# A two-layer hybrid decoder trunk in fp32: spacing of attention's units among the weight blocks of the input projection, 1.65 against 2.3 blocks

## The chip, the cores and the metric

The kernel runs on one core of a Trainium2 chip. Its engines are TensorE (PE: matrix products and transposes), VectorE (DVE), ScalarE (ACT), GpSimd (POOL) and SyncE (SP, which here issues DMAs). Each engine executes its own instructions in one fixed order and waits on semaphores where an operand comes from another engine. The metric is the device time of one execution, in microseconds, as the median of several runs.

## The reference

Input `x` is (1, 512, 1024) float32; two layers follow each other. Cut to what matters:

```python
h = rmsnorm(x, norm_mix)
z = h @ w_in     # columns: attention q | k | v, mLSTM q | k | v | o, i/f gates, branch gates A | B
att = sliding_window_attention(q_a, k_a, v_a, att_sinks)      # 8 heads, 2 key heads, window 128
hm  = rmsnorm(mlstm_chunkwise(q_m, k_m, v_m, i_pre, f_pre)) * sigmoid(o_m)
mixed = sigmoid(g_a) * (att @ w_att_branch) + sigmoid(g_m) * (hm @ w_m_branch)
x = x + mixed @ w_out
u = relu(rmsnorm(x, norm_ffn) @ w_ff1)
x = x + (u * u) @ w_ff2
```

Attention works in blocks of 128 queries, each of which sees its own and the previous block of keys. Queries and keys are normalised per head and turned by a partial rotary embedding; a learned sink joins each softmax. The mLSTM's decays come from the i and f gates; its queries and keys have 64 features per head, its values 128, with 4 heads.

## The kernel before, in words

**Products.** Everything is fp32. A large product is made of three matmuls in a faster format: each operand is split into a high and a low part, and high times high, high times low and low times high are added up in PSUM. A weight block is a 128 x 512 tile: SP loads it, ScalarE writes its high part (L165) and VectorE its low part (L166). There are three buffers for the raw block and four for the split one. `group_steps` runs one weight block against four PSUM banks of 128 x 512: four steps of a quarter block, three matmuls of 512 columns each, 12 matmuls to a block. All of PE's matmuls are recorded on L47 and all transposes on L52, since both go through small helpers. Products have five PSUM banks (`bank()`); all of attention's and the mLSTM's small products share three (`aux()`).

**The weave.** `weave(fill, side)` takes a list of fill steps with their widths in blocks, and a list of side steps with a time in blocks. It goes along the fill and, ahead of each step, issues the side steps that have come due. The framework's scheduler then takes this as the order of priority and fixes the order on each engine from dependencies, free buffers and its own estimate of durations; so an instruction can end up somewhat ahead of or behind its place in the list.

**The stretch that the change touches.** In the function `mixer` the second weave fills with nine groups of blocks: the mLSTM's queries and keys (0 to 8), branch gates 0 and 1 (8 to 16 and 16 to 24), the mLSTM's values V (24 to 32), the product of attention's result with its branch weights, called branch A (32 to 40), then two more gate groups around the mLSTM's output gate. Behind gate group 1 ScalarE makes eight sigmoids (L686) and reloads the table for exponentials (L692). Branch A is attention's first use.

The side holds attention as eight units, four query blocks b times two key heads kv. One unit consists of

- `att_scores(b, kv, hp)`, twice: four matmuls of 256 columns into an `aux` bank, copied out by ScalarE (L600; POOL's memset L598 for block 0) and VectorE (L601, a predicated copy that applies the mask). The first half is due at the unit's time, the second 1.25 blocks later;
- `att_softmax`, together with the second half: VectorE's maximum (L608 and L609), four exponentials on ScalarE with a sum (L614), the sink's (L616), then VectorE's sum, reciprocal and normalisation (L617, L618, L619);
- `att_probs`, 3.45 blocks after the unit's time: four transposes of the probabilities into an `aux` bank, split by ScalarE (L175) and VectorE (L176); for blocks above 0 POOL masks two copies (L634);
- `att_out`, 2.2 blocks after that: two or four matmuls of 512 columns, then ScalarE (L645, L652) and VectorE (L649, L653) write the high and low parts that branch A reads.

Keys and queries of the next block are transposed and split ahead of it: `k_tr` (one transpose; ScalarE L559 and L560, VectorE L561 and L562) and `q_tr` (four transposes; ScalarE L581, VectorE L582), timed back from the unit that first needs them. `qk_split` is the split of the mLSTM's queries and keys, eight times (ScalarE L673, POOL L675 and L677, VectorE L678 or L681). Four steps of the mLSTM's gating stand at 8.45, 11.45, 14.45 and 17.45, and the mLSTM's own steps follow from block 28 on. The first units read

```python
at = 7 + 1.65 * i
```

so units are due at 7, 8.65, ... 18.55, the last one's `att_out` at 24.2, and the last `qk_split` at 21.15.

Of the kernel before, what the change touches and what calls it, by code (L numbers as in the profile page):

```python
# [33 lines left out]
def hybrid_kernel(ctx, tc, x, norm_mix, w_in, att_q_norm, att_k_norm, att_sinks, m_gate_bias,  # L34
# [38 lines left out]
    def slot(dt=F32, shape=(P, T)):  # L73
        return now["act"].tile(list(shape), dt, tag="a", name=nm("a"))

    def temp(dt=F32):
        return now["tmp"].tile([P, T], dt, tag="t", name=nm("t"))
# [14 lines left out]
    def aux(shape=(P, T)):  # L92
        return now["paux"].tile(list(shape), F32, tag="aux", name=nm("aux"))
# [4 lines left out]
    def f32(ap):  # L98
        return ap.bitcast(F32)
# [288 lines left out]
    def mixer(l, norm, late, order, phase):  # L388
# [158 lines left out]
        def k_vec(b):  # L547
            rope(kvi[:, b, 0:128].rearrange("p (h d) -> p h d", d=HD), b, HKV)

        def k_tr(b):  # L550

            ps = aux([P, P])
            pe.transpose(ps, kvi[:, b, 0:128], ident)
            for h in range(HKV):
                r = slice(64 * h, 64 * h + 64)
                o = slice(64 - 64 * h, 128 - 64 * h)
                c = slice((b + 1) * P, (b + 2) * P)
                g = gcols[1][r, l:l + 1]
                sc.activation(kTh[r, h, c], ps[r, :], AF.Copy, scale=g)  # L559
                sc.activation(kTh[o, h, c], ps[r, :], AF.Copy, scale=g)  # L560
                ve.scalar_tensor_tensor(kTl[r, h, c], ps[r, :], g, f32(kTh[r, h, c]), op0=ALU.mult, op1=ALU.subtract)  # L561
                ve.tensor_copy(kTl[o, h, c], f32(kTl[r, h, c]))  # L562

        def q_vec(b):
            rope(q_tok[b].rearrange("p (h d) -> p h d", d=HD), b, HQ)

        def q_tr(b):


            ps = aux()  # L570
            for j in range(4):
                pe.transpose(ps[:, j * P:(j + 1) * P], q_tok[b][:, j * P:(j + 1) * P], ident)
            for j in range(2):
                qT[b, j] = temp(F32R)
                t4 = qT[b, j].rearrange("p (n i t) -> p n i t", n=2, i=2)
                p4 = ps[:, 2 * j * P:2 * (j + 1) * P].rearrange("p (n t) -> p n t", n=2)
                for i in range(2):
                    r = slice(64 * i, 64 * i + 64)
                    o = slice(64 - 64 * i, 128 - 64 * i)
                    g = gcols[0][r, l:l + 1]  # L580
                    sc.activation(t4[r, :, i, :], p4[r], AF.Copy, scale=g)  # L581
                    ve.scalar_tensor_tensor(t4[o, :, i, :], p4[r], g, f32(t4[r, :, i, :]), op0=ALU.mult,  # L582
                                            op1=ALU.subtract)

        def att_scores(b, kv, hp):
            if hp == 0:
                sps[b, kv] = temp()
            ps = aux()
            for i in range(2):
                c = 2 * hp + i  # L590
                lhs = qT[b, kv][:, c * P:(c + 1) * P]
                o = ps[:, i * 2 * P:(i + 1) * 2 * P]
                pe.matmul(o, lhs, kTh[:, kv, b * P:(b + 2) * P], start=True, stop=False)
                pe.matmul(o, lhs, kTl[:, kv, b * P:(b + 2) * P], start=False, stop=True)
            p4 = ps.rearrange("p (h w k) -> p h w k", h=2, w=2)
            dst = sps[b, kv][:, hp * 2 * P:(hp + 1) * 2 * P].rearrange("p (h k) -> p h k", h=2)
            if b == 0:
                gp.memset(dst, NEG)  # L598
            else:
                sc.activation(dst, p4[:, :, 0, :], AF.Copy)  # L600
            ve.copy_predicated(dst, tri_i.unsqueeze(1).to_broadcast([P, 2, P]), p4[:, :, 1, :])  # L601

        def att_softmax(b, kv):
            sp = sps[b, kv]
            s3 = sp.rearrange("p (h k) -> p h k", h=4)
            hs = slice(4 * kv, 4 * kv + 4)
            m = sm([P, 4], "m")
            ve.tensor_reduce(m, s3, axis=AX.X, op=ALU.max)  # L608
            ve.scalar_tensor_tensor(m, m, -1.0, nsinks[:, l, hs], op0=ALU.mult, op1=ALU.min)  # L609
            es = sm([P, 4], "es")  # L610
            ve.tensor_tensor(es, sinks[:, l, hs], m, op=ALU.add)
            den = sm([P, 4], "den")
            for i in range(4):
                sc.activation(s3[:, i, :], s3[:, i, :], AF.Exp, bias=m[:, i:i + 1],  # L614
                              accum_out=den[:, i:i + 1])
            sc.activation(es, es, AF.Exp)  # L616
            ve.tensor_tensor(den, den, es, op=ALU.add)  # L617
            ve.reciprocal(den, den)  # L618
            ve.tensor_tensor(s3, s3, den.unsqueeze(2).to_broadcast([P, 4, P]), op=ALU.mult)  # L619

        def att_probs(b, kv):
            sp = sps[b, kv]
            pt = aux()
            for i in range(4):
                pe.transpose(pt[:, i * P:(i + 1) * P], sp[:, i * P:(i + 1) * P], ident)
            hl = split(pt, get=lambda: temp(F32R))
            parts[b, kv] = [(hl, v2[:, 0, max(b - 1, 0), kv])]
            if b > 0:


                own = [temp(F32R) for _ in hl]
                for src, dst in zip(hl, own):
                    s3, d3 = (t.rearrange("p (h q) -> p h q", h=4) for t in (src, dst))
                    gp.affine_select(out=d3, in_=s3, compare_op=ALU.is_ge, fill=0.0, base=0,  # L634
                                     pattern=[[0, 4], [1, P]], channel_multiplier=-1)
                parts[b, kv].append((own, v2[:, 1, b - 1, kv]))
# [32 lines left out]
        def qk_split(m, i):  # L669
            t = qk_raw[m]  # L670
            r, o = slice(64 * i, 64 * i + 64), slice(64 - 64 * i, 128 - 64 * i)
            d = slot(F32R)
            sc.activation(d[r], t[r], AF.Copy)  # L673
            if m < 2:
                gp.tensor_copy(d[o], f32(d[r]))  # L675
                low = slot(F32R)
                gp.memset(f32(low[o]), 0.0)  # L677
                ve.tensor_tensor(low[r], t[r], f32(d[r]), op=ALU.subtract)  # L678
                m_q[2 * m + i], m_ql[2 * m + i] = d, low
            else:  # L680
                ve.tensor_tensor(d[o], t[r], f32(d[r]), op=ALU.subtract)  # L681
                m_k[2 * (m - 2) + i] = d
# [11 lines left out]
        def gate_steps(g, then=lambda: None):  # L694
            sg = []

            def ev(m, ps):
                sg.append(slot())
                ve.tensor_tensor(sg[m], ps, row[0], op=ALU.mult)  # L699
                if m == 3:  # L700
                    then()

            return sg, feat_steps(acts, wcols(C_G + 512 * g, 512), ev)
# [3 lines left out]
        def ev_v(b, ps):  # L707
            if b == 0:
# [5 lines left out]
        units = [(b, kv) for b in range(NB) for kv in range(HKV)]  # L714
        side = [(0, lambda: k_vec(0)), (0, lambda: q_vec(0)), (0, lambda: k_vec(1)), (0, lambda: q_vec(1)),
                (7 - 1.25, lambda: k_tr(0)), (7 - 1.75, lambda: q_tr(0))]
        for i, (b, kv) in enumerate(units):
            at = 7 + 1.65 * i
            side += [(at, lambda b=b, kv=kv: att_scores(b, kv, 0)),
                     (at + 1.25, lambda b=b, kv=kv: att_scores(b, kv, 1)),  # L720
                     (at + 1.25, lambda b=b, kv=kv: att_softmax(b, kv)),
                     (at + 3.45, lambda b=b, kv=kv: att_probs(b, kv)),
                     (at + 3.45 + 2.2, lambda b=b, kv=kv: att_out(b, kv))]
            if kv == 0 and b + 1 < NB:
                if b + 2 < NB:
                    side += [(at + 1, lambda b=b: k_vec(b + 2)), (at + 1, lambda b=b: q_vec(b + 2))]
                side += [(at + 2 * 1.65 - 1.75, lambda b=b: k_tr(b + 1)), (at + 2 * 1.65 - 2.15, lambda b=b: q_tr(b + 1))]
        side += [(8.45 + 3.0 * i, f) for i, f in enumerate((gating0, gating1, gating2, gating3))]
        side += [(9.6 + 1.65 * n, lambda n=n: qk_split(n // 2, n % 2)) for n in range(8)]
        g0, s0 = gate_steps(0)  # L730
        g1, s1 = gate_steps(1, lambda: back(sigmoid(g0 + g1)))

# [68 lines left out]
        for h in range(MH):  # L801
            at = 28 + 4.65 * h
# [568 lines left out]
```

## Time and profile before

| What | us |
| --- | --- |
| median of 3 runs | 1303.78 (1303.59 to 1304.21) |
| span of the profiled execution | 1302.9 |
| TensorE busy | 1291.5 |
| VectorE busy | 955.5 |
| ScalarE busy | 763.7 |
| GpSimd busy | 200.4 |
| layer 0, first unit's scores to branch A's first matmul | 66.47 to 163.01 |
| the same in layer 1 | 711.11 to 808.26 |

Times in rows of the trace are microseconds from the start of the span. A row in order of time has its start, its duration, the engine, the line, the operation, the tile written and the tiles read, the shape, the number of merged instructions, and in brackets the idle time ahead of it with what ended it. Matmuls are pipelined: the duration of one is longer than the distance to the next, so a wait of PE is read from start to start. A row of a group has busy time, mean duration in ns, and the idle time just before.

### The profile page before, as it was taken

How to read it: one execution, taken by the hardware profiler on the slowest of the kernel's cores; microseconds unless marked ns; L12 is line 12 of the kernel's file. 1: busy time of each engine (PE TensorE's matmuls, PEld its weight loads, DVE VectorE, ACT ScalarE, POOL GpSimd, SP SyncE). 2: the span in 40 equal slices, each digit the busy share in tenths (PEclk: the TensorE clock that was granted, in tenths of full speed). 3: DMA queues.
4: the chain of work that ended last, by engine and by line, in shares of the span. 5: the costliest groups of instructions: out<-in, count | busy, mean ns of one | idle time of the engine just before them, and what ended most of it. 6: DMA issues, size and time to landing. Idle time of an engine off the chain costs nothing. (4 is left out here: it accounts for less than half of the span.)

```text
span 1302.9 us, 19074 instructions
## 1 busy us (share of the span) xinstructions
PE 1291.5 (99%) x6978; PEld 1105.2 (85%) x6978; DVE 955.5 (73%) x1505; ACT 763.7 (59%) x1329; POOL 200.4 (15%) x281
## 2 busy tenths in 40 slices
PE   9999999999999999999999999999999999999998
PEld 6877788888889999999888778888888899999987
DVE  4699754475677897968948996545737878879797
ACT  5578755544466665656555787554445556665563
POOL 4511100000003021131115111000000030311210
PEclk9999999999999999999999999999999999999999
DMA  5422222372369888898124222223714597988953
GB/s 154 110 72 59 74 81 74 90 249 82 98 155 172 236 185 207 195 211 216 33 75 114 65 66 75 79 75 92 256 57 129 141 215 195 201 212 196 213 148 98
DMA packets 130542, 177.61 MB, mean 136 GB/s; under 512 B 9864, under 2 KB 78320, under 8 KB 130448
## 3 DMA queue, kind: packets, MB, share of 16 engines
q1 hardware_dynamic: 94208, 131.82, 32.7%
q0 software_dynamic: 35520, 44.17, 21.2%
q8 instruction: 55, 0.90, 0.3%
q10 hardware_dynamic: 720, 0.40, 0.1%
q14 instruction: 39, 0.32, 0.1%
HBM read 174.27 MB, written 2.10 MB: 135 GB/s over the span
## 5 line engine op out<-in xcount | busy, mean ns | idle before, releaser
L47 PE MATMUL mm<-i,wh 128*128 128x512 f32 (+1 forms) x1280 | 352.7, 362 | 0.0
L867 ACT ACTIVATE wh<-raw 128x1024 fp32r<-128x1024 f32 x212 | 223.1, 1056 | 181.1 <-PE mm L47 114.0
L868 DVE TENSOR_TENSOR wl<-raw,wh 128x1024 fp32r<-128x1024 f32 x212 | 255.2, 1218 | 74.2 <-ACT wh L867 72.3
L47 PEld LDWEIGHTS mm<-i,wh 128*128 128x128 f32 x1280 | 224.3, 189 | 32.1 <-DVE a L699 0.8
L166 DVE TENSOR_TENSOR wl<-w,wh 128x512 fp32r<-128x512 f32 (+1 forms) x208 | 140.8, 679 | 137.7 <-ACT wh L165 129.4
L47 PE MATMUL mm<-i,wl 128*128 128x512 f32 (+1 forms) x640 | 229.8, 360 | 0.0
L165 ACT ACTIVATE wh<-w 128x512 fp32r<-128x512 f32 (+1 forms) x208 | 127.0, 611 | 146.7 <-PE mm L47 122.8
L47 PE MATMUL mm<-wh,uh 128*128 128x512 f32 x440 | 171.8, 390 | 0.0
L47 PE MATMUL mm<-wl,uh 128*128 128x512 f32 x440 | 171.7, 390 | 0.0
L47 PE MATMUL mm<-wh,ul 128*128 128x512 f32 x440 | 171.2, 389 | 0.0
L1027 POOL DMA_DIRECT2D raw<-in_w_ff_dram x48 | 62.3, 1304 | 591.3 <-DMA raw<-in_w_ff_dram 316.9
L47 PE MATMUL mm<-wh,i 128*128 128x512 f32 (+1 forms) x512 | 150.6, 370 | 1.2 <-ACT wh L165 0.6
L47 PEld LDWEIGHTS mm<-i,wl 128*128 128x128 f32 x640 | 120.8, 189 | 18.1 <-DVE wl L868 0.4
L47 PEld LDWEIGHTS mm<-wh,i 128*128 128x128 f32 x512 | 92.0, 188 | 19.0 <-DVE i L179 2.1
L913 DVE SCALAR_TENSOR_TENSOR x<-mm,ms,x 128x512 f32<-128x512 f32 x126 | 90.4, 743 | 9.9 <-PE mm L47 9.9
L47 PEld LDWEIGHTS mm<-wh,ul 128*128 128x128 f32 x440 | 82.6, 188 | 17.4
L47 PEld LDWEIGHTS mm<-wh,uh 128*128 128x128 f32 x440 | 82.8, 188 | 16.1
L47 PEld LDWEIGHTS mm<-wl,uh 128*128 128x128 f32 x440 | 82.8, 188 | 15.6
L47 PE MATMUL mm<-wl,i 128*128 128x512 f32 (+1 forms) x256 | 93.0, 363 | 0.0
L47 PE MATMUL mm<-wh,a 128*128 128x512 f32 x256 | 81.3, 392 | 0.0
L47 PE MATMUL mm<-a,wh 128*128 128x512 f32 x256 | 80.5, 397 | 0.0
L47 PE MATMUL aux<-i,wh 128*128 128x256 f32 x384 | 69.5, 283 | 0.0
(259 smaller groups left out, 2161.0 us busy)
## 6 DMA issues: line engine op xcount, KB each, us to landing
raw<-in_w_ff_dram SPq DMA_DIRECT2D x144, 512.0 KB, 5.2
raw<-in_w_ff_dram POOLq DMA_DIRECT2D x84, 512.0 KB, 7.8
w<-in_w_in_dram SPq DMA_DIRECT2D x128, 256.0 KB, 2.6
w<-in_w_out_dram SPq DMA_DIRECT2D x32, 256.0 KB, 2.7
w<-in_w_att_branch_dram SPq DMA_DIRECT2D x16, 256.0 KB, 2.6
w<-in_w_m_branch_dram SPq DMA_DIRECT2D x16, 256.0 KB, 2.7
w<-in_w_in_dram SPq DMA_DIRECT2D x16, 128.0 KB, 2.1
out_dram<-x SPq DMA_DIRECT2D x7, 256.0 KB, 2.0
```

Source lines behind the costliest of these rows:

```text
L47: latest[0] = nc.tensor.matmul(*args, **kw)
L165: sc.activation(wh[:, :off], raw[:, :off], AF.Copy)
L166: ve.tensor_tensor(wl[:, :off], raw[:, :off], f32(wh[:, :off]), op=ALU.subtract)
L867: sc.activation(hi, src, AF.Copy)
L868: ve.tensor_tensor(lo, src, f32(hi), op=ALU.subtract)
L913: ve.scalar_tensor_tensor(xh[:, cc], ps[i][:, cc], ms[j][:, b:b + 1], xh[:, cc], op0=ALU.mult, op1=ALU.add)
L1027: gp.dma_start(to[h], src(h, i, j), accum_op=ALU.add)
```

## The change

One number is made a variable and set to 2.3. It is used in three places: the distance from unit to unit, the times of the next block's `k_tr` and `q_tr` (which are counted back from that block's first unit), and the distance of the eight `qk_split` steps. Within a unit the offsets stay (1.25, 3.45 and 5.65 blocks), and so do the first unit's time, the gating steps and everything of the mLSTM from block 28 on.

```diff
                 (7 - 1.25, lambda: k_tr(0)), (7 - 1.75, lambda: q_tr(0))]
+        pace = 2.3
         for i, (b, kv) in enumerate(units):
-            at = 7 + 1.65 * i
+            at = 7 + pace * i
             side += [(at, lambda b=b, kv=kv: att_scores(b, kv, 0)),
                      (at + 1.25, lambda b=b, kv=kv: att_scores(b, kv, 1)),
                      (at + 1.25, lambda b=b, kv=kv: att_softmax(b, kv)),
...
-                side += [(at + 2 * 1.65 - 1.75, lambda b=b: k_tr(b + 1)), (at + 2 * 1.65 - 2.15, lambda b=b: q_tr(b + 1))]
+                side += [(at + 2 * pace - 1.75, lambda b=b: k_tr(b + 1)), (at + 2 * pace - 2.15, lambda b=b: q_tr(b + 1))]
         side += [(8.45 + 3.0 * i, f) for i, f in enumerate((gating0, gating1, gating2, gating3))]
-        side += [(9.6 + 1.65 * n, lambda n=n: qk_split(n // 2, n % 2)) for n in range(8)]
+        side += [(9.6 + pace * n, lambda n=n: qk_split(n // 2, n % 2)) for n in range(8)]
```

After it units are due at 7, 9.3, 11.6, 13.9, 16.2, 18.5, 20.8 and 23.1, the last one's `att_out` at 28.75 and the last `qk_split` at 25.7; branch A still begins at block 32. In the changed file the lines behind L717 have numbers higher by one.

## The prediction

> **What bounds the kernel now.** I read the page's totals and clock first, then the table of stages, then TensorE's instructions in order of time, and last the groups of VectorE and ScalarE in the stretch where attention runs.
>
> ```profile
> span 1302.9 us, 19074 instructions
> PE 1291.5 (99%) x6978; PEld 1105.2 (85%) x6978; DVE 955.5 (73%) x1505; ACT 763.7 (59%) x1329; POOL 200.4 (15%) x281
> PEclk9999999999999999999999999999999999999999
> ```
>
> TensorE is the bound nearly everywhere, at the full granted clock. The change adds no instruction (their number is the same on every engine), so it can move the time only by making TensorE's waits shorter or longer. The waits are small: where attention runs, the stages read (time, then each engine's busy time, then the granted clock, 1.00):
>
> ```profile
> 66.47:163.01 96.54, 94.42 (x466) 74.72 (x464) 82.50 (x204) 75.53 (x201) 16.47 (x29) 1.00 0.25 69
> 70.73:136.18 65.45, 63.33 (x323) 49.34 (x322) 60.50 (x152) 52.40 (x142) 10.73 (x17) 1.00 0.24 65
> 136.18:163.01 26.83, 26.83 (x123) 21.79 (x121) 17.92 (x45) 21.29 (x57) 4.02 (x7) 1.00 0.24 71
> 711.11:808.26 97.15, 94.38 (x466) 74.69 (x464) 82.94 (x203) 75.66 (x201) 15.94 (x29) 1.00 0.25 69
> ```
>
> The first row runs from the first unit's scores to branch A's first matmul in layer 0, the last is the same stretch of layer 1. Rows two and three split layer 0 where the group of the mLSTM's values (V, fill blocks 24 to 32) begins: up to there VectorE is busy 60.50 of 65.45 us (0.92), after it 17.92 of 26.83 (0.67). So VectorE, in order and nearly full, is late for TensorE before V and has room in V. The waits themselves:
>
> ```profile
> 72.67 0.27 PE L52 MATMUL aux<-ident,kvi 128*128 128x128 f32 x1
> 73.62 0.72 PE L47 MATMUL aux<-kT,t 128*128 128x256 f32 x4 [0.69 <-ACT t L581]
> ...
> 80.66 0.63 PE L47 MATMUL mm<-i,wh 128*128 128x512 f32 x2
> 81.48 0.63 PE L52 MATMUL aux<-ident,t 128*128 128x128 f32 x4 [0.20 <-DVE t L619]
> ...
> 90.78 0.39 PE L47 MATMUL mm<-i,wh 128*128 128x512 f32 x1
> 91.18 0.65 PE L52 MATMUL aux<-ident,t 128*128 128x128 f32 x4
> ...
> 121.93 0.39 PE L47 MATMUL mm<-i,wh 128*128 128x512 f32 x1
> 122.49 0.66 PE L52 MATMUL aux<-ident,t 128*128 128x128 f32 x4 [0.17 <-DVE t L601]
> ...
> 130.59 0.39 PE L47 MATMUL mm<-i,wl 128*128 128x512 f32 x1
> 131.54 0.63 PE L52 MATMUL aux<-ident,t 128*128 128x128 f32 x4 [0.56 <-ACT wh L165]
> ...
> 142.07 0.61 PE L47 MATMUL mm<-wh,i 128*128 128x512 f32 x2
> 142.75 0.61 PE L47 MATMUL mm<-wh,i 128*128 128x512 f32 x2
> ...
> 144.11 0.61 PE L47 MATMUL mm<-wh,i 128*128 128x512 f32 x2
> 144.71 0.63 PE L52 MATMUL aux<-ident,t 128*128 128x128 f32 x4
> ...
> 717.31 0.27 PE L52 MATMUL aux<-ident,kvi 128*128 128x128 f32 x1
> 718.87 0.71 PE L47 MATMUL aux<-kT,t 128*128 128x256 f32 x4 [1.29 <-ACT t L581]
> ...
> 725.87 0.63 PE L47 MATMUL mm<-i,wh 128*128 128x512 f32 x2
> 726.73 0.52 PE L52 MATMUL aux<-ident,t 128*128 128x128 f32 x3 [0.23 <-DVE t L619]
> ...
> 775.83 0.39 PE L47 MATMUL mm<-i,wl 128*128 128x512 f32 x1
> 776.78 0.63 PE L52 MATMUL aux<-ident,t 128*128 128x128 f32 x4 [0.56 <-ACT wh L165]
> ```
>
> Three 512-wide matmuls take 142.75 - 142.07 = 0.68 us, 0.228 each; a 128-wide transpose starts its successor after about 0.11. A wait is what start to start holds beyond that. 72.67 to 73.62 is 0.95 - 0.11 = 0.84 (1.45 in layer 1), where unit 1's first scores need the PSUM bank that q_tr(1)'s conversions still read. 80.66 to 81.48 is 0.82 - 0.46 = 0.36 (0.40), unit 0's transposes behind its normalisation L619. 130.59 to 131.54 is 0.95 - 0.23 = 0.72 (0.72), unit 5's transposes, with ScalarE's queue named as what they waited for. From 90.78 to 123.30 stand ten more of 0.12 to 0.33 (the first 0.40 - 0.23 = 0.17, the last but one 0.56 - 0.23 = 0.33, the longest), 2.3 us; layer 1 has eleven, 2.5 us. V holds one wait, at unit 6's transposes: 144.11 to 144.71 is 0.60 - 0.46 = 0.14. Smaller steps at changes of matmul form, about 2.1 us a layer, belong to counts that stay.
>
> **The change, part by part.** Instructions are moved on PE, VectorE, ScalarE and POOL, from unit 0's second scores to the end of V, in both layers alike. SP's DMA order is the same, so no transfer moves to another place in a queue; weight tiles are split four buffers ahead, and a late split would show only beyond that cover, which I price at zero.
>
> In the order that the changed program has, units' first scores stand at fill blocks 2.2, 4.7, 6.9, 9.2, 11.9, 16.0, 18.3, 22.3, counted with V at 19.2 to 27.2, where they stood at 2.2, 3.9, 5.7, 7.8, 9.3, 14.3, 16.0, 17.1. So behind V's start now stand also unit 5's transposes, unit 6's second scores, and all of unit 7.
>
> (a) q_tr(1) is now issued behind unit 1's first scores, so they no longer wait for its conversions: -0.84 in layer 0, -1.45 in layer 1.
> (b) Unit 0's transposes have fewer of VectorE's instructions ahead of them (one unit and block 1's conversions later): -0.36, -0.40.
> (c) Unit 5's transposes leave that crowded place: -0.72 each. They then stand in V behind the return of the activation table, priced in (f).
> (d) The other early waits. k_tr(b), q_tr(b) and the qk splits move too, so new neighbours come: unit 1's second scores stand right behind k_tr(1)'s conversion, unit 4's transposes behind k_tr(3)'s. Going along the new order, these waits come to about 2.7 where they were 2.3 and 2.5, an estimate from the durations of the groups: +0.3. From below: half go, -1.2. From above: each of the ten as long as the longest, 0.33, is 3.3: +1.0.
> (e) Unit 1's transposes come 6.6 us after its second scores (28 matmuls and what is between). How long is a unit's chain from second scores to normalised probabilities? Two measured ones, and the bare sum:
>
> ```profile
> 71.28 0.63 PE L47 MATMUL mm<-i,wh 128*128 128x512 f32 x2
> 78.10 0.63 PE L47 MATMUL mm<-i,wh 128*128 128x512 f32 x2
> ```
> ```profile
> 80.66 0.68 DVE L619 TENSOR_TENSOR t<-t,den 128x512 f32<-128x512 f32 x1
> 84.89 0.69 DVE L619 TENSOR_TENSOR t<-t,den 128x512 f32<-128x512 f32 x1
> ```
> ```profile
> L601 DVE COPY_PREDICATED t<-tri_l,aux 128x256 f32<-128x256 int32 x16 | 6.8, 442 | 0.2
> L619 DVE TENSOR_TENSOR t<-t,den 128x512 f32<-128x512 f32 x8 | 5.5, 686 | 0.1
> L176 DVE TENSOR_TENSOR t<-aux,t 128x512 fp32r<-128x512 f32 x8 | 5.5, 684 | 0.2
> L608 DVE TENSOR_REDUCE m<-t 128x4 f32<-128x512 f32 x8 | 5.4, 680 | 0.2
> L681 DVE TENSOR_TENSOR a<-a,a 64x512 fp32r<-64x512 f32 x4 | 3.2, 798 | 0.1
> ```
> ```profile
> 76.48 0.40 ACT L614 ACTIVATE t<-t,m 128x128 f32<-128x128 f32 x1
> 78.03 0.61 ACT L165 ACTIVATE wh<-w 128x512 fp32r<-128x512 f32 x1
> ```
>
> Unit 0's runs from 71.28 to 81.34 (10.1 us), unit 1's from 78.10 to 85.58 (7.5). Bare it is 0.44 + 0.68 + the four exponentials 1.55 (76.48 to 78.03) + 0.69 and about 0.8 for four short ones: 4.2. I take 0.3 here, between zero and 7.5 - 6.6 = 0.9.
>
> (f) **The tail in V.** Unit 6's and unit 7's second scores and transposes stand 28 matmuls apart: 28 x 0.228 = 6.4 us of cover. V's share of VectorE grows by two L608, two L601, an L619, L176, L681 and small ones, 5.2 us: (17.92 + 5.2) / 26.83 = 0.86, near the 0.92 under which unit 1's chain took 7.5. So I take 7.5: 1.1 us of wait for each, 2.2 a layer. Ends: 4.2 gives no wait; unit 0's 10.1 gives 3.7 each. Unit 5's transposes stand 3.2 blocks after V's start, behind the sigmoids and the table:
>
> ```profile
> 139.75 1.28 ACT L692 ACT_TABLE_LOAD   x1
> ```
> ```profile
> L634 POOL TENSOR_SCALAR_AFFINE_SELECT t<-t 128x512 fp32r<-128x512 f32 x12 | 8.9, 740 | 54.3 <-ACT t L175 38.8 <-DVE kT L561 13.4 <-DVE t L176 1.7
> ```
>
> Exponentials from 139.75 + 1.28 on, with 1.55 for themselves, 0.69 for L619 and some 0.5 of short ones, end at 143.8; 3.2 blocks of 12 matmuls behind 136.18 is 144.9. That leaves 1.1 us, and a weight split and unit 4's evacuation share ScalarE's queue there: +0.4 (0 to 1). The last products follow their transposes by a few matmuls and need two selects, 2 x 0.74 us, behind a split of 0.6: +0.6 over three units (0 to 1.2). The mLSTM's first steps follow directly: +0.3. With the 0.14 of before gone, the tail is +3.4.
> (g) First use: branch A reads unit 7's tiles only in its third weight block, 24 matmuls (5.5 us) after its start, and what stands between are seven evacuating instructions on ScalarE and VectorE, none longer than the 0.68 of L176: under 4.8, so no wait; if the cover went, that is the price.
>
> **Sum.** Layer 0: -0.84 - 0.36 - 0.72 + 0.3 + 0.3 + 3.4 = +2.1. Layer 1: -1.45 - 0.40 - 0.72 + 0.3 + 0.3 + 3.4 = +1.4. Span 1302.9 + 3.5 = 1306.4. The median of the runs, 1303.78, stands 0.88 above the profiled span, so 1307.3.
>
> A rule that speaks against the change: the Trainium skill, "TensorE: Matmul & The Clock Gate", section "HAM oscillation", warns of idle gaps of TensorE longer than about 3.4 us, after which its clock is halved. Here the longest wait, 1.45 us, left the granted clock at 1.00; by the trace the tail's waits cost themselves alone, by the rule the same as long as none reaches 3.4. Where a chain like unit 0's made waits of 3.7 (the last rival but one), an estimate by that page is one window of 3.4 us at half rate after each, 1.7 more, 7 for four; no wait here is long enough to show it.
>
> **The rivals.** *Faster.* VectorE is relieved before V and V's chains run at 6.4 us or less, because 0.86 leaves gaps: the two tail waits of 1.1 vanish, the rest of the tail is about 0.4, and half of the early waits of (d) go: -1.9 - 1.2 + 0.1 + 0.4 = -2.6 in layer 0 (0.1 is what is left of (e)) and -2.6 - 1.2 + 0.1 + 0.4 = -3.3 in layer 1: 1303.78 - 5.9 = 1297.9. For it: the bare 4.2, and 0.67 in V. It decides from a chain under 6.4 us. *Same.* Chains near 6.9: tail waits of 0.5 each, 1.2 a layer less than mine: 1307.3 - 2.4 = 1304.9. *Much slower.* Chains like unit 0's: +2.6 for four waits, 1307.3 + 10.4 = 1317.7; against it, unit 0's chain stood behind q_tr(1)'s conversions, which V has not. *The pace does not arrive:* the program's order already puts units 2.0 to 4.1 blocks apart, not 2.3, since banks and engines' estimates place them; this is in the positions used above. Had the order come out as before, the time would be 1303.8; it did not.
>
> **How the numbers follow.** Slower as forecast, or more, 0.50; same, 0.28; faster, 0.22. I count 0.2% (2.6 us) as about what can be told from no change. The range, 1299 to 1312, reaches down to most of the faster case (half of (d)'s gain missing: 1303.78 - 4.7 = 1299.1) and up to the middle between the forecast and the much slower case (1312), to which I leave 0.05 of the 0.50.
>
> **What would show it.** Right: no wait at unit 1's first scores; waits of about 1 us for L619 at the transposes of units 6 and 7 within V; V longer than 26.83 by some 3 us; the stretch before V shorter by about 1.5 to 2.5 us. Wrong: V at 27 us, chains there under 6.4; or new waits before V as large as those removed; or branch A waiting for L653.

## The result and the profile after

The changed kernel takes 1306.76 us (median of 10 runs, 1306.37 to 1307.3), the kernel before 1303.73 (10 runs): a ratio of 1.0023, 95% interval 1.0014 to 1.0032, so 3.0 us slower (1.8 to 4.2 by the interval). 1307.3 was forecast, with a range of 1299 to 1312.

The page's totals of the changed kernel, and its stages (time, then the busy time of PE, weight loads, VectorE, ScalarE and POOL, the granted clock):

```profile
span 1305.1 us, 19082 instructions
PE 1291.4 (99%) x6978; PEld 1105.1 (85%) x6978; DVE 954.1 (73%) x1505; ACT 762.6 (58%) x1329; POOL 198.4 (15%) x281
```
```profile
69.80:133.93 64.13, 60.73 (x307) 47.92 (x307) 55.80 (x141) 48.16 (x128) 8.35 (x12) 1.00 0.24 66
133.93:163.61 29.68, 29.33 (x139) 23.03 (x138) 19.60 (x51) 21.96 (x62) 3.96 (x7) 1.00 0.24 72
65.60:163.61 98.01, 94.27 (x466) 74.53 (x465) 79.47 (x199) 72.03 (x192) 14.38 (x26) 1.00 0.25 71
711.92:809.94 98.02, 94.34 (x465) 74.51 (x464) 79.47 (x197) 71.83 (x192) 14.41 (x26) 1.00 0.25 70
```

PE's busy time is that of before, and so is the number of instructions on every engine; the eight more in the total are semaphore instructions. The stretch from the first unit's scores to branch A is 98.01 us in layer 0 instead of 96.54, and 98.02 instead of 97.15 in layer 1: 2.3 of the 3.0 us. (The two spans differ by 2.2 only, since the profiled execution of before reached its first unit 0.9 us later, ahead of every moved instruction.) Another 0.7 us stands behind the stretches, 0.2 behind layer 0's and 0.5 behind layer 1's; of this the first products of the mLSTM behind branch A's start hold 0.2 and 0.3 as waits.

TensorE's work in this stretch is about 89.9 us a layer at the start-to-start distances of undisturbed rows: 300 products by 0.228, 31 small ones of 512 columns by 0.230, 64 of 256 by 0.120, 51 transposes by 0.108, and 1.2 for the rest. What is beyond that is waiting or change of form. It is named "excess" below, split where V begins:

| excess, us | layer 0 ahead of V | layer 0 in V | layer 1 ahead of V | layer 1 in V |
| --- | --- | --- | --- | --- |
| before | 6.32 | 0.28 | 6.93 | 0.28 |
| after | 6.82 | 1.26 | 6.79 | 1.30 |

So the growth, net, is 2.0 us in V and 0.4 ahead of it, both layers together; ahead of V, new waits came about as large as those that went.

TensorE of the changed kernel in order of time, layer 0. The first three rows show the place where no wait is left; each group behind it ends in a row that waited:

```profile
72.72 0.62 PE L47 MATMUL mm<-i,wh 128*128 128x512 f32 x2
73.17 0.39 PE L47 MATMUL mm<-i,wl 128*128 128x512 f32 x1
73.39 0.64 PE L47 MATMUL aux<-kT,t 128*128 128x256 f32 x4
...
79.25 0.40 PE L47 MATMUL mm<-i,wh 128*128 128x512 f32 x1
80.82 0.72 PE L47 MATMUL aux<-kT,t 128*128 128x256 f32 x4 [1.17 <-DVE kT L561]
...
99.11 0.39 PE L47 MATMUL mm<-i,wl 128*128 128x512 f32 x1
100.20 0.71 PE L47 MATMUL aux<-t,v 128*128 128x512 f32 x2 [0.70 <-DVE kT L561]
...
126.47 0.61 PE L47 MATMUL mm<-i,wh 128*128 128x512 f32 x2
127.87 0.63 PE L52 MATMUL aux<-ident,t 128*128 128x128 f32 x4 [0.78 <-DVE kT L561]
...
142.33 0.39 PE L47 MATMUL mm<-wl,i 128*128 128x512 f32 x1
142.90 0.63 PE L52 MATMUL aux<-ident,t 128*128 128x128 f32 x4 [0.18 <-DVE t L619]
143.29 1.20 PE L47 MATMUL aux<-kT,t 128*128 128x256 f32 x8
...
150.07 0.39 PE L47 MATMUL mm<-wh,i 128*128 128x512 f32 x1
150.54 0.63 PE L52 MATMUL aux<-ident,t 128*128 128x128 f32 x4
```

Unit 1's first scores (73.39) follow without a wait. Then 79.25 to 80.82 is 1.57 - 0.23 = 1.34 at unit 1's second scores, 99.11 to 100.20 is 0.86 at unit 1's products, 126.47 to 127.87 is 0.94 at unit 4's transposes: 3.1 us in three places, in both layers alike. In V the transposes of units 5, 6 and 7 wait 0.35, 0.24 and 0.24.

VectorE tells what ended the three early waits; the first rows are its queue ahead of the first of them:

```profile
76.57 0.69 DVE L619 TENSOR_TENSOR t<-t,den 128x512 f32<-128x512 f32 x1
77.29 0.48 DVE L582 SCALAR_TENSOR_TENSOR t<-aux,gc,t 64x256 fp32r<-64x256 f32 x1
77.80 0.69 DVE L166 TENSOR_TENSOR wl<-w,wh 128x512 fp32r<-128x512 f32 x1
78.52 0.49 DVE L582 SCALAR_TENSOR_TENSOR t<-aux,gc,t 64x256 fp32r<-64x256 f32 x1
79.05 0.34 DVE L561 SCALAR_TENSOR_TENSOR kT<-aux,gc,kT 64x128 fp32r<-64x128 f32 x1
79.42 0.22 DVE L562 CAST kT<-kT 64x128 fp32r<-64x128 f32 x1
79.56 0.47 DVE L582 SCALAR_TENSOR_TENSOR t<-aux,gc,t 64x256 fp32r<-64x256 f32 x1
80.32 0.36 DVE L561 SCALAR_TENSOR_TENSOR kT<-aux,gc,kT 64x128 fp32r<-64x128 f32 x1 [0.28 <-ACT kT L560]
80.71 0.22 DVE L562 CAST kT<-kT 64x128 fp32r<-64x128 f32 x1
...
127.37 0.36 DVE L561 SCALAR_TENSOR_TENSOR kT<-aux,gc,kT 64x128 fp32r<-64x128 f32 x1
...
149.71 0.69 DVE L619 TENSOR_TENSOR t<-t,den 128x512 f32<-128x512 f32 x1
```

k_tr(1)'s transpose began at 75.69, but its conversions come behind unit 0's normalisation (L619), a weight split (L166) and q_tr's own conversions (L582), so the second L561 ends only at 80.68. It is the last reader of k_tr's PSUM bank. TensorE goes on 0.14 us after its end (80.68, then 80.82; 127.73, then 127.87) and doesn't wait for L562, which still writes the keys. So at that instant it is the bank that is missing. The last row ends unit 6's chain: its second scores are the first four of the eight that begin at 143.29 and are over at 143.8, the normalisation ends at 150.40, 6.6 us later.

### The profile page after: what moved, and what is told of

It is laid out like the page before. It is cut to its first block, busy times and chain, and to the rows that moved or that the text cites. A ratio compares the mean times of both kernels' runs of the same rounds, so it can differ in the third digit from the quotient of the medians.

```text
span 1305.1 us, 19082 instructions
## 1 busy us (share of the span) xinstructions
PE 1291.4 (99%) x6978; PEld 1105.1 (85%) x6978; DVE 954.1 (73%) x1505; ACT 762.6 (58%) x1329; POOL 198.4 (15%) x281
## 4 chain that ended last, share of the span: by engine, by line
PE 94%; DVE 3%; ACT 2%; issue 1%; DMA 1%; DVEq 0%; SPq 0%; ACTq 0%
PE mm L47 76%; PE aux L47 15%; PE aux L52 2%; DVE wl L166 1%; ACT t L614 1%; DVE t L582 1%; ACT wh L165 0%; DMA w<-in_w_in_dram 0%; DVE a L681 0%; DVE kT L561 0%; DVE t L619 0%; DMA x<-in_x_dram 0%; ACT t L581 0%; DVE t L649 0%; DVE t L474 0%
## 5 line engine op out<-in xcount | busy, mean ns | idle before, releaser
L166 DVE TENSOR_TENSOR wl<-w,wh 128x512 fp32r<-128x512 f32 (+1 forms) x208 | 142.0, 685 | 135.7 <-ACT wh L165 127.5
L165 ACT ACTIVATE wh<-w 128x512 fp32r<-128x512 f32 (+1 forms) x208 | 127.2, 612 | 144.2 <-PE mm L47 114.2
```

The costliest lines, as they stand in the source:

```text
L165: sc.activation(wh[:, :off], raw[:, :off], AF.Copy)
L166: ve.tensor_tensor(wl[:, :off], raw[:, :off], f32(wh[:, :off]), op=ALU.subtract)
```

## The experiments

All were timed in five rounds beside the kernel before. The table has the difference of the medians (of before, on the same chip), and the excess of both layers together, which carries more than half of each difference of over 1 us. By the 95% intervals a difference is known to about 1.2 us either way (1.6 to 1.8 for the units alone and the two runs with four banks), so 1.6, 1.8 and 3.0 are not clearly apart.

| run | time against before, us | excess ahead of V | excess in V |
| --- | --- | --- | --- |
| before | | 13.25 | 0.56 |
| the change | +3.0 | 13.61 | 2.56 |
| units alone | +4.8 | 11.41 | 6.00 |
| qk_split alone | -1.8 | 11.68 | 0.63 |
| k_tr, q_tr at their old distance | +1.6 | 12.71 | 2.14 |
| q_tr's loops swapped | +1.8 | 13.07 | 2.27 |
| units 0 to 4 spread | +0.8 | 11.26 | 3.13 |
| units 4 to 7 spread | +1.6 | 12.11 | 2.90 |
| pace 2.0 | +3.1 | 13.95 | 1.70 |
| qk_split alone, loops swapped | -1.1 | 11.58 | 0.62 |
| qk_split from block 13 on | -0.1 | 11.41 | 1.49 |
| qk_split from 10.6 on | -0.6 | 11.76 | 0.70 |
| the change, four banks | +8.6 | 16.12 | 3.82 |
| before, four banks | +5.5 | 15.15 | 2.04 |

**The parts alone.** Units with k_tr and q_tr at 2.3, qk_split back at 1.65; and then, in the kernel before, the splits alone at 2.3.

```diff
-        side += [(9.6 + pace * n, lambda n=n: qk_split(n // 2, n % 2)) for n in range(8)]
+        side += [(9.6 + 1.65 * n, lambda n=n: qk_split(n // 2, n % 2)) for n in range(8)]
```

> Units, k_tr and q_tr at 2.3 blocks as in the changed kernel, the eight qk_split back at 1.65. Theory A (the added time is TensorE waiting ahead of V for the next block's conversions of keys and queries, k_tr and q_tr, which now stand directly ahead of a unit's small products): the waits stay, 1306 to 1308 us, with a wait of about 1.3 us at unit 1's second scores in both layers. Theory B (the prediction's main term, the tail in V): V still holds its three waits, 1306.8. Theory C (the moved qk_split): back at 1303.7.

```diff
-        side += [(9.6 + 1.65 * n, lambda n=n: qk_split(n // 2, n % 2)) for n in range(8)]
+        side += [(9.6 + 2.3 * n, lambda n=n: qk_split(n // 2, n % 2)) for n in range(8)]
```

> Only the eight qk_split at 2.3 blocks, all else as before. Theory A and B: 1303.0 to 1304.5 us, TensorE's waits ahead of V as before (4.2 and 5.0 us in the two layers). Theory C: 1306 to 1307.

The units alone: 1309.1 us (ratio 1.0038, 1.0025 to 1.0051). The splits alone: 1302.49 against 1304.28 (0.9986, 0.9978 to 0.9995), faster than both kernels. +4.8 and -1.8 make the +3.0 of the whole. No theory gave the time of either run: the change is a loss and a gain in one. Theory A's wait at unit 1's second scores is there (1.33 us in both layers), yet the excess ahead of V is 1.8 less than before. The units' loss lies in V, where the forecast had put it, and the largest piece is this, on TensorE and ScalarE of layer 0 of the run with the units alone:

```profile
159.83 0.39 PE L47 MATMUL mm<-wh,i 128*128 128x512 f32 x1
162.16 0.63 PE L52 MATMUL aux<-ident,t 128*128 128x128 f32 x4 [1.94 <-DVE t L619]
```
```profile
158.44 0.39 ACT L614 ACTIVATE t<-t,m 128x128 f32<-128x128 f32 x1
...
158.95 1.85 ACT L711 ACTIVATE vm<-mm,ncol 128x512 f32<-128x512 f32 x3
160.67 0.22 ACT L616 ACTIVATE es<-es 128x4 f32<-128x4 f32 x1
```

Unit 7's transposes wait 2.33 - 0.23 = 2.1 us (1.9 in layer 1). They stand one block later than in the changed kernel, and there V's own evacuation (L711, three in a row, 1.85 us) comes ahead of the sink's exponential (L616) in ScalarE's queue; the sum, reciprocal and normalisation wait behind it.

**The conversions' place.** The next block's k_tr and q_tr go back to their old distance from their unit, all else as changed.

```diff
-                side += [(at + 2 * pace - 1.75, lambda b=b: k_tr(b + 1)), (at + 2 * pace - 2.15, lambda b=b: q_tr(b + 1))]
+                side += [(at + 2 * 1.65 - 1.75, lambda b=b: k_tr(b + 1)), (at + 2 * 1.65 - 2.15, lambda b=b: q_tr(b + 1))]
```

> Units and qk_split at 2.3, but the next block's k_tr and q_tr at the times of before (1.55 and 1.15 blocks behind their unit, not 2.85 and 2.45), so there is 1.25 blocks of products between q_tr(1) and unit 1's first scores. Theory A: the wait of 1.3 us at unit 1's second scores goes and the other two behind k_tr shrink, 1303 to 1305 us; V is as in the changed kernel. Theory B and C: 1306.8, as the changed kernel.

1305.92 us (ratio 1.0013, 1.0004 to 1.0022), about 1.4 of the 3.0 gone: above Theory A's range and below what B and C gave. What TensorE waited for in layer 0, with the total, the number and the longest, in the changed kernel and in this run:

```profile
PE aux L47 <- DVE kT L561: 1.9, 2, 1.2
PE aux L52 <- DVE kT L561: 0.8, 1, 0.8
```
```profile
PE aux L52 <- DVE t L619: 1.4, 2, 1.2
PE aux L47 <- DVE t L582: 0.6, 1, 0.6
PE aux L52 <- ACT wh L165: 0.6, 1, 0.6
```

The waits for L561 are gone, as expected: 1.34, 0.86 and 0.6 us less at the three places of each layer. But unit 0's transposes now wait 1.34 for their normalisation, and three later products 0.5 to 0.8 each. Of about 5.6 us that went in the two layers, 1.4 arrives in the time: the conversions' place is part of the cause, not all.

**A shorter conversion.** q_tr's loops swapped, in the changed kernel:

```diff
             for j in range(2):
                 qT[b, j] = temp(F32R)
-                t4 = ...
-                for i in range(2):
+            for i in range(2):
+                for j in range(2):
+                    t4 = ...
```

> The changed kernel with the two loops of q_tr swapped: the first half of both tiles is converted, then the second, so ScalarE's next conversion does not follow directly on a VectorE conversion of the same tile. TensorE's order stays the same. Theory A: q_tr's conversion chain of about 4.5 us gets about 1 us shorter, the waits behind it fall by 0.5 to 1 us each in three places of each layer, 1303.5 to 1305.5 us. Theory B and C: 1306.8.

1306.03 against 1304.28 (ratio 1.0015, 1.0006 to 1.0023): 1.8 more than before and 1.3 less than the change cost, but with waits of 1.21, 0.95 and 1.11 us at the same three places. The swap did not make the conversions shorter, as it was meant to: from the start of k_tr(1)'s transpose to the end of its last L561 it is 4.85 us (75.63 to 80.48), with the old loops 4.99 (75.69 to 80.68). So the alternation of ScalarE and VectorE in q_tr is not what makes them long, and what shorter conversions would give is not shown. Together with the moved splits at the old pace the swap gave nothing:

> Only the eight qk_split at 2.3 blocks, all else of the old pace, and the loops of q_tr swapped. Theory A: the gain of the first (1.8 us) and part of what the swap gave at the pace 2.3 (1.3 us) add: 1300.8 to 1302.2 against 1304.0 of before. If the swap only shifts the waits: 1302.0 to 1302.8.

1302.47 us against 1303.58 (ratio 0.9991, 0.9982 to 0.9999), the same time as with the moved splits alone, but by the kernel before on the same chip a gain of 1.1 instead of 1.8.

**A bank more.** Four PSUM banks for the small products and four for the large ones, in the changed kernel and in the one before.

```diff
-    psum_pools(start, 3)
+    psum_pools(start, 4, 4)          # small, large; was 3 and 5
...
-                psum_pools(phase, 3)
+                psum_pools(phase, 4, 4)
```

> The changed kernel with four PSUM banks for attention's and the mLSTM's small products instead of three, and four for the large products instead of five, in both layers. Theory A, made narrower by the first four runs (a small product waits until k_tr's VectorE conversion L561 has let go of the third bank): the three waits of 1.34, 0.86 and 0.94 us that end at L561 vanish or fall under 0.3; the large products' groups may pay for their lost bank, 0 to 1 us at each of some ten group boundaries a layer, so the time is 1302 to 1312, and the difference to the next run, the same banks at the old pace, is under 1.5 us where it is 3.0 with three banks. Rival B (conversions and softmax are late for TensorE whatever the banks): waits of the same size at the same places, the difference to the next run stays at 3.

> The kernel before with the same four and four banks. Theory A: its waits at unit 1's first scores (0.84 and 1.45 us) vanish as well; 1301 to 1312 us, depending on what the large products pay. Rival B: those waits stay.

1312.15 and 1309.08 us: the difference stays 3.1, as the rival said, and both are slower than with three and five. But the named waits do not stay, as the rival had it: those at unit 1's second scores (1.34) and products (0.86) are gone in the changed kernel, those at unit 1's first scores (0.84 and 1.45) in the kernel before. Only unit 4's transposes still wait, 1.0, now behind their normalisation. Layer 0 of the changed kernel with four banks, where this file's lines are higher by one (L562 is L561 above, L620 is L619, L166 is L165, L700 is the evacuation L699):

```profile
78.71 0.40 PE L47 MATMUL mm<-i,wl 128*128 128x512 f32 x1
78.94 0.64 PE L47 MATMUL aux<-kT,t 128*128 128x256 f32 x4
```
```profile
80.70 0.36 DVE L562 SCALAR_TENSOR_TENSOR kT<-aux,gc,kT 64x128 fp32r<-64x128 f32 x1 [0.28 <-ACT kT L561]
```

Unit 1's second scores (78.94) follow without a wait, 2.1 us before k_tr(1)'s last reader ends (81.06), though that reader is as late behind the transpose as with three banks (5.0 us). So at this place the third bank, held by a late conversion, was what TensorE waited for. Other waits came instead; the longest in layer 0:

```profile
PE mm L47 <- DVE a L700: 1.0, 1, 1.0
PE aux L52 <- ACT wh L166: 1.0, 1, 1.0
PE aux L52 <- DVE t L620: 0.8, 1, 0.8
PE aux L52 <- DVE kT L562: 0.7, 1, 0.7
```

The first is a large product that waits for one of its own banks to be emptied, which is the price of the bank given away. The others are transposes. With a bank more the scheduler issues the later small products earlier (unit 7's transposes two blocks earlier), and they meet VectorE and ScalarE still late there. As the order moved and the large products lost a bank, these runs compare two plans; they do not show what a bank more alone would give.

**Which units.** The spread of the first units with the old end, and the old start with a late end; qk_split at 2.3 in both, k_tr and q_tr counted back from the first unit of their block.

```diff
-            at = 7 + pace * i
+            at = starts[i]       # [7, 9.3, 11.6, 13.9, 16.2, 17.0, 17.8, 18.55]
                                  # or [7, 8.65, 10.3, 11.95, 14.7, 17.5, 20.3, 23.1]
```

> The qk_split at 2.3 as in the changed kernel; units 0 to 4 at its times (7 to 16.2), units 5 to 7 pressed together to 17, 17.8 and 18.55, so that the last unit is due when it was before. If the added time comes ahead of V, from the spread of the first units (1.34 at unit 1's second scores, 0.86 at unit 1's products): those two waits stay, V keeps under 0.4 us of waits, and the time is 1305.5 to 1307. If it comes from the tail: 1302 to 1303.5, near the kernel with the moved splits alone.

> The qk_split at 2.3; units 0 to 3 at the times of before (1.65 apart), units 4 to 7 at 14.7, 17.5, 20.3 and 23.1, so that the last unit is due as in the changed kernel. If the added time comes ahead of V: the wait at unit 1's first scores of before is there (0.8 to 1.4), those of the changed kernel at unit 1's second scores and products are not, V has about 1 us of waits a layer, and the time is 1303 to 1305. If it comes from the tail: 1306 to 1308.

1304.35 us (ratio 1.0004, 0.9995 to 1.0013) and 1305.06 (1.0012, 1.0003 to 1.0021), 0.8 and 1.6 more than before. The first lies between its two ranges, the second at the edge of one: neither half alone has the whole cost. Against the splits alone (-1.8), which these two contain, they cost 2.6 and 3.4 (differences between two chips, each known to about 1.2 us), and in both V takes 2.3 to 2.5 of it: 0.63 grows to 3.13 and 2.90. In the first the waits of 1.34 and 0.86 are there as in the changed kernel, but the later ones ahead of V are less, so their sum is that of the splits alone. Its units 5 to 7 were due early, and yet the program's order has their transposes in V.

**The size of the step.** The whole change with 2.0.

```diff
-        pace = 2.3
+        pace = 2.0
```

> The whole change with 2.0 blocks instead of 2.3. If the cost grows evenly with the pace: (2.0 - 1.65) / 0.65 of 3.0 us, 1305.4. If it hangs on which products the conversions happen to stand ahead of (here q_tr(1) ahead of unit 1's first scores, with 1.8 blocks between k_tr(1) and the second scores, so that the wait of 1.34 goes; but seven products close before V), no even step: 1302.5 to 1305 with other waits.

1306.58 us (ratio 1.0023, 1.0014 to 1.0032), 3.1 more than before, as much as at 2.3, and more than the even step or the other guess gave: a cost proportional to the pace would be 1.6, just below the interval's 1.8. Other waits make it up: in layer 0 1.33 at unit 1's second scores, which were expected to go without it, 1.05 and 0.73 at two later scores.

**Where the splits gain.** All else as before, the splits 2.0 apart from block 13, or 2.3 apart from 10.6.

```diff
-        side += [(9.6 + 1.65 * n, lambda n=n: qk_split(n // 2, n % 2)) for n in range(8)]
+        side += [(13.0 + 2.0 * n, lambda n=n: qk_split(n // 2, n % 2)) for n in range(8)]
```

> All else as before, the eight qk_split from block 13 on, 2.0 blocks apart (the last at 27). If the gain of spreading them is that VectorE has fewer 0.7 us subtractions while it converts block 1's queries and keys, moving all of them behind that gains as much or more: 1300.5 to 1302.5, with the wait at unit 1's first scores under 0.5 us in both layers. If the gain is elsewhere: 1303 to 1305.

> The old pace for the units, the eight qk_split 2.3 apart from 10.6 on (9.6 with the first of these runs, which gained 1.8; from 13 on gained nothing). If one block more takes the 1.0 us wait at unit 1's first scores away and adds no other: 1301 to 1302.3. If the waits only change place: 1302.5 to 1304.

1303.46 against 1303.58 (0.9999, 0.999 to 1.0008) and 1302.88 against 1303.51 (0.9996, 0.9987 to 1.0005): neither can be told from no change. From block 13 on, the wait at unit 1's first scores falls from 0.85 and 1.45 to 0.13, as expected; but a wait of 1.0 comes up at unit 4's transposes and 0.4 in V. From 10.6 on, unit 1's first scores still wait 0.92, and unit 0's transposes 0.85 instead of 0.37. With the splits 2.3 apart from 9.6, TensorE in layer 0 reads

```profile
72.04 0.27 PE L52 MATMUL aux<-ident,kvi 128*128 128x128 f32 x1
73.14 0.72 PE L47 MATMUL aux<-kT,t 128*128 128x256 f32 x4 [0.83 <-ACT t L581]
```

so there the wait at unit 1's first scores is still 0.99 in layer 0; layer 1 lost 0.7 of its 1.45, and the rest of the gain is in smaller steps. That version, 1.8 us faster than before (0.7 to 2.9 by the interval), is the best found. Why its place among these three matters is not shown: with the splits from block 13 on, VectorE has none of them while it converts block 1's queries and keys, and the time did not fall clear of noise.

## Why the prediction was right, and where it was not

Sign and size were right: +3.5 was summed, +3.0 measured. The sum was of the two stretches, which grew by 2.3; the other 0.7 it did not have. (It also put 0.88 between the profiled span and the median; in the changed kernel that is 1306.76 - 1305.1 = 1.66, since the profiled execution of before reached its first unit late.) By stages it was not right: ahead of V it had 3.3 us less for both layers together, and the excess there grew by 0.4; in V it had 6.8 more, and it grew by 2.0. The terms, per layer, by the pieces of the trace:

- (a) right: no wait at unit 1's first scores, -0.84 and -1.45. But the wait for a bank came back at unit 1's second scores, 1.34, which belongs to (d).
- (b) half: unit 0's transposes still wait 0.21, so -0.15 and -0.19 instead of -0.36 and -0.40.
- (c) right: the 0.72 ahead of V is gone; unit 5 waits 0.35 in V, where 0.4 was put.
- (d) mis-sized, by far: +0.3 was taken, +1.0 was its upper end. Without the waits of (a) to (c), the large steps ahead of V were 2.3 and 2.4 us and are now 5.1 in both layers; 0.2 of that is (e), so (d) is about +2.5. Of the three waits behind k_tr two were foreseen in place (unit 1's second scores and unit 4's transposes, not unit 1's products), none in length: the upper end allowed 0.33 each, and they are 0.86 to 1.34. At the first, by the rows above, the conversion stood behind a normalisation, a weight split and q_tr's own conversions, and the bank was not free before its end.
- (e) right: 0.22 against 0.3.
- (f) mis-sized the other way: V's excess grew by 1.0 a layer, not by 3.4. The chain took 6.6 us there, not 7.5, against 6.4 us of cover and the products between: 0.24 a unit instead of 1.1. That is the nearest to the rival "same", whose chain was 6.9. The 7.5 rested on VectorE 0.86 busy in V; it was 19.60 of 29.68 us, 0.66. The moved units brought about 4.3 us of VectorE's work into V in layer 0, near the 5.2 that were summed, but 2.3 us left it, mainly two multiplications of the mLSTM (L760) and two of the low parts that branch A reads (L653), which now come behind branch A's start; and V itself grew longer. The products' selects cost next to nothing in V; the mLSTM's start, +0.3 in the sum, cost 0.2 and 0.3 behind it.

Steps at changes of form ahead of V fell by about 0.5 a layer and rose by 0.3 in V, which the sum had left out. So two errors of about 2.3 us a layer, (d) and (f), took each other away: that the total came so near is luck, with the waits in another place than it said. And one step was missing: the moved qk_split, put into (d) without a price, is a gain of 1.8 us, and the units alone a loss of 4.8.

Of what was to show it: no wait at unit 1's first scores, right. Waits of about 1 us for the normalisation at units 6 and 7, wrong (0.24), though the run with the units alone had 2.1 at unit 7. V longer by some 3 us, right by the row (29.68 against 26.83), but 1.9 of these 2.9 are the sixteen small matmuls that moved into it (12 of 0.12, 4 of 0.11). The stretch ahead of V is then shorter by 1.4 and 2.0 (68.34 and 68.30 against 69.71 and 70.32), and again 1.9 of it are these matmuls, which that sign had not allowed for. One sign of being wrong was there too: new waits before V, larger than those removed. The clock stayed at 1.00 in every stage, also around the wait of 2.1 in the run with the units alone. No wait came near the 3.4 us of which the Trainium skill, "TensorE: Matmul & The Clock Gate", section "HAM oscillation", speaks, so its rule stays untested here.

What stays open is why the excess ahead of V stays between 11.3 and 14.0 us for two layers in every plan with three banks, though waits of 0.9 to 1.4 us were removed from it one after the other. The scheduler, which places each small product by its own estimate of the engines ahead of it, would do that if the estimate is short of the real chains; no run here isolates it. Open, too, is why the units' spacing and the splits' spacing add up as they do: with the splits moved as well, unit 7's transposes stand one block earlier and the wait of 2.1 is gone, but why the scheduler puts them there is not shown.

## What to carry to other kernels

Where TensorE is 99% busy and small products wait in its fixed order, moving their due times mostly moved the waits here: price each moved product by all that stands in VectorE's and ScalarE's queue ahead of what it needs, also of what frees its bank, and not by its own conversion. A stage that grows because instructions moved into it has not become slower; take the moved work off first. When one number drives several things, measure them apart: here one of two was a gain.

## What the runs showed that was not expected

A bank taken from the large products and given to the small ones cost 5.5 us (1309.08 against 1303.58), of which 3.4 are excess in the two stretches (17.2 against 13.8). The bank removed most of the waits that it was meant for, and others came in their place. And some 1.8 us of this kernel hung on when the eight qk_split of a layer are issued, each with one subtraction of 0.7 to 0.8 us on VectorE, which is 73% busy over the span but 0.92 ahead of V; that VectorE's part of the split is what counts is not shown.
